# Hybrid decoder trunk on one core: the prompt's keys turned by token with VectorE blocks and small DMAs, final states at the end of each scan

## The chip, the cores and the metric

The kernel runs on one core of one Trainium2 chip. A core has five engines with a program each: TensorE (PE in the profile, its weight loads PEld), VectorE (DVE), ScalarE (ACT), GpSimd (POOL) and SyncE (SP). SP computes nothing here and only issues DMAs. The engines wait for each other and for DMAs through semaphores. The metric is the device time of one execution in microseconds (us), lower being better.

## The reference

One inference step of a single decoder layer, for a prompt of 256 tokens and for a group of 8 samples with 4 new tokens each (32 columns), so 288 tokens of width 2048 in fp32:

```python
x = x + 0.5 * rmsnorm(swiglu(rmsnorm(x, g[0]), ffn1_w_in, ffn1_w_out), g[1])
m, sg, sh = hybrid_mixer(rmsnorm(x, g[2]), ...)
x = x + rmsnorm(m, g[3])
x = x + 0.5 * rmsnorm(swiglu(rmsnorm(x, g[4]), ffn2_w_in, ffn2_w_out), g[5])
```

The mixer projects its input to the queries, keys, values and gates of 4 GLA heads (key width 128, value width 256) and 8 HGRN heads (128 and 128). Each head is a recurrence over the tokens with a decay per key element:

```python
# S_t = diag(exp(log_a_t)) S_{t-1} + k_t^T v_t ; o_t = q_t S_t
s_new = (jnp.exp(last)[..., None] * s
         + jnp.einsum('bhsd,bhsv->bhdv', ki * jnp.exp(last - cum), vi))
```

The prompt starts from a zero state and the samples from states that are read from memory. Outputs are the 288 tokens, the state of every head after the prompt, and the 8 new states of every head for the samples. For this document the second line matters: a head's state after the prompt is the product, over all 256 tokens, of the keys (each scaled by the decay from its token to the end) with the values.

## The kernel before

Nearly all of the time goes into products of weights with 288 columns. `Weights` loads every weight matrix once, in units of 128 x 1024 fp32 (512 KB), through SP into three buffers `raw`. ACT rounds a unit to fp32r (`wh`, L95) and DVE forms the rest (`wl`, L96). With the input split the same way into `xh` and `xl`, `block` makes three products of 128x128 weights with 288 columns for each piece: `xh*wh` (L520), `xl*wh` (L521), `xh*wl` (L522). Loads and splits run ahead of PE: three units may be loaded and four split before PE comes to them.

In the mixer a second stream of work lies between these products. `block` calls `tick` once for each of the 16 row tiles k of its input, and each tick takes one step of the oldest unfinished `scan`, a generator whose steps end at its `yield` statements. There are six scans of two heads each: two GLA scans, then four HGRN scans. A scan lies between the products of the blocks qk, v, hfq, hi and gate, as its ticks fall. The scheduler of the language may move an instruction within its engine's order a little; each engine then works strictly in that order.

A scan holds two heads a = 0, 1 with their queries, keys `k` (128 key elements on the partitions, 288 tokens along the row) and decay. In eight levels DVE multiplies decays into `k` and `Q` in place (`update`, L961 and L964), PE makes scores (L919 to L1017) and DVE or ACT put them into `Dg`. After the last level `k` holds each prompt key scaled to the end of the prompt. Then the second part begins, which the change touches:

- `key_t(a)` (L1085) turns the keys of head a: PE transposes the 256 prompt tokens in two products with the identity (L828) and the 32 sample tokens, kept three times side by side in `K3`, in a third (L829), all into one PSUM tile `tp_k`. PSUM tiles of this kind (`auxtile`) have three buffers.
- `key_e(a)` (L1090): ACT copies the prompt part to `kd`, which has tokens on the partitions (L1094), and ACT and DVE split the sample part to `ks` (L833, L835).
- `out(a)`: the prompt's output from scores and values (L1113 to L1117).
- for every nb samples `halve`, `apart` and `sample`: a state tile `s` is loaded by SP (L895, five buffers), split, multiplied by the queries (L1159), updated on DVE (L1163, from the product `sn`, L1151 or L1154) and stored by POOL (`out_dram<-s`, L1165).
- `final(a)` (L1121): the state after the prompt, two products of `kd` with the values (L1126), copied by ACT to `st` (one buffer, L1128) and stored by POOL (L1129). It is called in head a's first sample step.
- `inter_a`, `inter_b` (with the product `os<-sel`, L1177), `norm_a` and later `norm_b`, `norm_c` finish the outputs of a head.

POOL has little to do in this stretch: it issues the stores of `s` and `st`. SP's queue holds the weight loads and the loads of `s`, in one order; a load of `s` waits until the store of the tile five before it has landed. At the very end of the program the last FFN already turns tiles with DVE's 32x32 block transpose (`turn32`, L625, L627) and moves the blocks into place with DMAs (`move32`, L636, L640), issued by POOL and SP.

Of the kernel before, what the change touches and what calls it, by code (L numbers as in the profile page):

```python
# [9 lines left out]
F32 = mybir.dt.float32  # L10
# [6 lines left out]
P = 128  # L17
# [20 lines left out]
class Weights:  # L38
# [77 lines left out]
    def next(self):  # L116
        if self.used >= self.split:
            self.ahead()
        p = self.parts.pop(self.used)
        self.used += 1  # L120
        return p
# [3 lines left out]
def trunk_kernel(ctx, tc, x_prompt, x_sample, state_gla, state_hgrn, norm_gains, f1_in, f1_out, f2_in, f2_out,  # L125
# [615 lines left out]
    def mixer(pn, border):  # L741
        with ExitStack() as mx:
# [82 lines left out]
            def by_token(tp, src, src3):  # L825

                for t in range(2):
                    PE.transpose(tp[:, t * P:(t + 1) * P], src[:, t * P:(t + 1) * P], ident)  # L828
                PE.transpose(tp[0:96, TP:TP + P], src3, ident)  # L829
# [42 lines left out]
            def scan(d, Vt, V32, Vs, gla, ytile0, s0, sp_out, ss_out):  # L872
# [209 lines left out]
                put(LEVELS - 1, pss.pop(LEVELS - 1))  # L1082
                kds, bds, hls, sqs, pos, mss = {}, {}, {}, {}, {}, {}

                def key_t(a):  # L1085
                    tp = auxtile("tp_k")
                    by_token(tp, k[:, a, :], K3[:, a].rearrange("p n t -> p (n t)"))
                    return tp

                def key_e(a, tp):  # L1090

                    kd = sp[0].tile([P, 2, P], F32, name="kd", tag="kd")
                    ks = sp[0].tile([96, P], F32R, name="ks", tag="ks")
                    S.activation(kd, tp[:, 0:TP].rearrange("p (t c) -> p t c", c=P), AF.Copy)  # L1094
                    stack(ks, tp, 2 * TS)
                    kds[a] = kd, ks

                def apart(a, b0):

# [6 lines left out]
                def out(a):  # L1106
                    vc = Vt[:, :, a * dv:(a + 1) * dv]

                    po, ss = auxtile("o"), auxtile("os")
                    for j in range(nv):  # L1110
                        vj = vc[:, :, j * P:(j + 1) * P]
                        c0, c1, c2 = j * TP, j * TP + P, (j + 1) * TP
                        PE.matmul(po[:, c0:c1], vj[:, 0, :], Dg[:, 0, a, :], start=j == 0, stop=True, skip_group_check=True)  # L1113
                        PE.matmul(po[:, c1:c2], vj[:, 0, :], X[:, a, :], start=False, stop=False, skip_group_check=True)
                        PE.matmul(po[:, c1:c2], vj[:, 1, :], Dg[:, 1, a, :], start=False, stop=True, skip_group_check=True)
                        c0 = TP + j * TS
                        PE.matmul(ss[:, c0:c0 + TS], V32[:, a * dv + j * P:a * dv + (j + 1) * P], Ds[:, a, :],  # L1117
                                  start=j == 0, stop=False, skip_group_check=True)
                    pos[a] = po, ss

                def final(a):  # L1121

                    kd, vc = kds[a][0], Vt[:, :, a * dv:(a + 1) * dv]
                    ps = auxtile("st")
                    for t in range(2):
                        PE.matmul(ps[:, 0:dv], kd[:, t, :], vc[:, t, :], start=t == 0, stop=t == 1)  # L1126
                    st = tmp.tile([P, dv], F32, name="st", tag="st", bufs=1)
                    S.activation(st, ps[:, 0:dv], AF.Copy)  # L1128
                    G.dma_start(sp_out[a], st)  # L1129

                def halve(a, b0):

                    load_state()
                    s = states[a, b0]
                    for i in range(2):
                        hl = sp[0].tile([P, 512], F32R, name="hl", tag="hl", bufs=4)
                        v = hl.rearrange("p (b two c) -> p b two c", two=2, c=dv)
                        sv = s[:, i * nb // 2:(i + 1) * nb // 2, :]
                        with tc.issue_after(pn.behind[1]), tc.issue_after(pn.behind[2]):
                            S.activation(v[:, :, 0, :], sv, AF.Copy)  # L1140
                            V.tensor_tensor(v[:, :, 1, :], sv, v[:, :, 0, :].bitcast(F32), op=ALU.subtract)
                        hls.setdefault((a, b0), []).append(hl)
# [24 lines left out]
                def inter_a(a):  # L1167
                    ss = pos[a][1]
                    it = its[0]
                    S.activation(it[0:2 * TS, 0:dv], ss[0:2 * TS, 0:dv], AF.Copy)  # L1170
                    if not gla:
                        V.tensor_tensor(it[0:2 * TS, 0:dv], it[0:2 * TS, 0:dv], ss[0:2 * TS, dv:2 * dv], op=ALU.add)
# [7 lines left out]
                def norm_a(a):  # L1180
                    for j in range(nv):
                        yt = y[ytile0 + a * nv + j]
                        S.activation(yt[:, 0:TP], pos[a][0][:, j * TP:(j + 1) * TP], AF.Copy)
                        S.activation(yt[:, TP:T], pos[a][1][:, TP + j * TS:TP + (j + 1) * TS], AF.Copy)
                        sq = sqp.tile([P, T], F32, name="hsq", tag="sq")
                        S.activation(sq, yt, AF.Square)
                        if j == 1:
                            V.tensor_tensor(sq, sq, sqs[a], op=ALU.add)
                        sqs[a] = sq
                    h = sqp.tile([P, T], F32R, name="nh", tag="pn")  # L1190
                    l = sqp.tile([P, T], F32R, name="nl", tag="pn")
                    S.activation(h, sqs[a], AF.Copy)
                    V.tensor_tensor(l, sqs[a], h.bitcast(F32), op=ALU.subtract)
                    sqs[a] = h, l
# [18 lines left out]
                                               op0=ALU.mult, op1=ALU.mult)  # L1213

                tp = key_t(0)
                halve(0, 0)
                yield
                out(0)
                key_e(0, tp)
                apart(0, 0)  # L1220
                yield
                for a in range(2):
                    for b0 in range(0, NB, nb):
                        if b0 + nb < NB:
                            apart(a, b0 + nb)
                            halve(a, b0 + nb)
                        if b0 == 0:
                            final(a)
                        sample(a, b0)
                        if a == 0 and b0 == nb:  # L1230
                            tp = key_t(1)
                        yield
                        if a == 0 and b0 == nb:
                            key_e(1, tp)
                    if a == 0:
                        apart(1, 0)
                        halve(1, 0)
                    inter_a(a)
                    yield
                    inter_b(a)  # L1240
                    norm_a(a)
                    later.append([lambda: None, lambda: None, lambda a=a: norm_b(a), lambda a=a: norm_c(a)])
                    yield
                    if a == 0:
                        out(1)
                        yield

            gens, later = [], []
# [228 lines left out]
```

## Time and profile before

| what | us |
|---|---|
| median of three runs | 2281.41 (2281.22 to 2283.21) |
| the profiled execution | 2280.79 |
| its span from first to last instruction | 2279.0 |
| PE busy | 2264.1 (99%) |
| DVE busy | 1420.8 (62%) |
| ACT busy | 1034.4 (45%) |
| POOL busy | 115.8 (5%) |

The profile is one execution of the program, and its times count from its first instruction. Busy time is the union of an engine's instructions; matmuls overlap, since one starts while the one before it still runs, so the distance from start to start tells what a matmul costs, and its duration does not. A row of a group gives the number of its instructions behind an x. Waits are put down to what ended them. "DMA to landing" is the time from a DMA's issue until its data and its semaphore have arrived. The scans lie between about 918 and 1280 us.

### The profile page before, as it was taken

The numbers are of one execution on the slowest core, as the hardware profiler recorded it, in microseconds if no ns is written. First come the engines' busy times: TensorE is split into PE (matmuls) and PEld (weight loads), VectorE is DVE, ScalarE is ACT, GpSimd is POOL, SyncE is SP. The second block draws the span as 40 slices with busy tenths as digits, with TensorE's granted clock in tenths as the row PEclk, the third lists the DMA queues.
The fourth block names the chain that finished last, engine by engine and source line by source line (L and its number), as shares of the span: only waits on it lengthen the run. The fifth ranks groups of instructions, "written<-read, shape, count | busy, mean of one in ns | idle before, by whom it ended". The sixth has DMA issues, their size and how long they took to land.

```text
span 2279.0 us, 42090 instructions
## 1 busy us (share of the span) xinstructions
PE 2264.1 (99%) x17164; PEld 2252.0 (99%) x17164; DVE 1420.8 (62%) x2375; ACT 1034.4 (45%) x1603; POOL 115.8 (5%) x204
## 2 busy tenths in 40 slices
PE   9999999999999999999999999999999999999998
PEld 9999999999999999999999999999999999999997
DVE  7545545554555468889889754954555455545546
ACT  6443333333334346556656654644333333333344
POOL 0000000000000002001000000260000000000003
PEclk9999999999999999999999999999999999999999
DMA  7555555555555545456465554475555555555555
GB/s 218 169 165 165 165 167 165 166 166 167 167 167 185 166 158 163 139 171 198 144 183 159 167 183 160 141 203 169 165 166 164 166 167 166 167 167 167 167 163 151
DMA packets 228801, 382.42 MB, mean 168 GB/s; under 512 B 24018, under 2 KB 63936, under 8 KB 228608
## 3 DMA queue, kind: packets, MB, share of 16 engines
q1 hardware_dynamic: 219088, 366.27, 50.7%
q0 software_dynamic: 7344, 13.29, 2.1%
q8 instruction: 134, 2.20, 0.4%
q10 hardware_dynamic: 2176, 0.18, 0.1%
q14 instruction: 59, 0.48, 0.1%
HBM read 363.75 MB, written 11.80 MB: 165 GB/s over the span
## 4 chain that ended last, share of the span: by engine, by line
PE 94%; DVE 3%; DMA 1%; ACT 1%; issue 0%; DVEq 0%; SPq 0%; ACTq 0%
PE gate L522 9%; PE gate L520 9%; PE gate L521 9%; PE up L522 8%; PE up L520 8%; PE up L521 8%; PE out L521 8%; PE out L522 8%; PE out L520 8%; PE hfq L520 2%; PE hfq L522 2%; PE mo L522 1%; PE mo L520 1%; PE mo L521 1%; PE hfq L521 1%; PE v L520 1%
## 5 line engine op out<-in xcount | busy, mean ns | idle before, releaser
L96 DVE TENSOR_TENSOR wl<-raw,wh 128x1024 fp32r<-128x1024 f32 (+1 forms) x674 | 821.6, 1219 | 621.0 <-ACT wh L95 619.1
L95 ACT ACTIVATE wh<-raw 128x1024 fp32r<-128x1024 f32 (+1 forms) x674 | 711.6, 1057 | 1017.6 <-PE gate L521 315.8
L522 PE MATMUL gate<-xh,wl 128*128 128x288 f32 x1660 | 489.0, 295 | 0.2 <-DVE wl L96 0.2
L520 PE MATMUL gate<-xh,wh 128*128 128x288 f32 x1660 | 488.9, 296 | 0.3 <-ACT wh L95 0.3
L521 PE MATMUL gate<-xl,wh 128*128 128x288 f32 x1660 | 485.5, 295 | 0.0
L522 PE MATMUL out<-hh,wl 128*128 128x288 f32 x1408 | 415.1, 295 | 0.9 <-DVE wl L96 0.9
L521 PE MATMUL out<-hl,wh 128*128 128x288 f32 x1408 | 415.7, 295 | 0.0
L522 PE MATMUL up<-xh,wl 128*128 128x288 f32 x1408 | 415.0, 295 | 0.0
L520 PE MATMUL up<-xh,wh 128*128 128x288 f32 x1408 | 414.8, 295 | 0.1
L521 PE MATMUL up<-xl,wh 128*128 128x288 f32 x1408 | 414.6, 294 | 0.0
L520 PE MATMUL out<-hh,wh 128*128 128x288 f32 x1408 | 413.7, 294 | 0.0
L522 PEld LDWEIGHTS gate<-xh,wl 128*128 128x128 f32 x1660 | 311.5, 188 | 0.6 <-DVE wl L96 0.6
L520 PEld LDWEIGHTS gate<-xh,wh 128*128 128x128 f32 x1660 | 310.9, 188 | 1.2 <-ACT wh L95 0.5
L521 PEld LDWEIGHTS gate<-xl,wh 128*128 128x128 f32 x1660 | 310.4, 188 | 0.2
L522 PEld LDWEIGHTS out<-hh,wl 128*128 128x128 f32 x1408 | 264.7, 188 | 1.1 <-DVE wl L96 1.1
L520 PEld LDWEIGHTS out<-hh,wh 128*128 128x128 f32 x1408 | 264.6, 188 | 0.0
L520 PEld LDWEIGHTS up<-xh,wh 128*128 128x128 f32 x1408 | 264.1, 188 | 0.5 <-ACT g L590 0.3
L521 PEld LDWEIGHTS out<-hl,wh 128*128 128x128 f32 x1408 | 264.4, 188 | 0.0
L521 PEld LDWEIGHTS up<-xl,wh 128*128 128x128 f32 x1408 | 264.2, 188 | 0.1
L522 PEld LDWEIGHTS up<-xh,wl 128*128 128x128 f32 x1408 | 264.2, 188 | 0.0
L671 DVE TENSOR_TENSOR y<-out,y 128x288 f32<-128x288 f32 x288 | 121.4, 452 | 98.9 <-PE out L522 95.9
L520 PE MATMUL hfq<-xh,wh 128*128 128x288 f32 x256 | 77.5, 303 | 0.0
(381 smaller groups left out, 2598.2 us busy)
## 6 DMA issues: line engine op xcount, KB each, us to landing
raw<-in_ffn_w_in_dram SPq DMA_DIRECT2D x351, 512.0 KB, 3.4
raw<-in_ffn_w_out_dram SPq DMA_DIRECT2D x176, 512.0 KB, 3.5
raw<-in_mix_w_in_dram SPq DMA_DIRECT2D x64, 512.0 KB, 3.7
raw<-in_mix_w_in_dram SPq DMA_DIRECT2D x96, 256.0 KB, 3.2
raw<-in_mix_w_out_dram SPq DMA_DIRECT2D x32, 512.0 KB, 3.7
out_dram<-s POOLq DMA_DIRECT2D x32, 256.0 KB, 3.5
s<-in_state_gla_dram SPq DMA_DIRECT2D x16, 256.0 KB, 4.2
s<-in_state_hgrn_dram SPq DMA_DIRECT2D x16, 256.0 KB, 3.6
```

The lines of the kernel that those rows point to most:

```text
L95: i1 = self.nc.scalar.activation(h[:, c], raw[:, c], AF.Copy).ins
L96: i2 = self.nc.vector.tensor_tensor(l[:, c], raw[:, c], h[:, c].bitcast(F32), op=ALU.subtract).ins
L520: yield lambda: PE.matmul(dst, w[0][:, c:c + P], parts[0], start=start, stop=False)
L521: yield lambda: PE.matmul(dst, w[0][:, c:c + P], parts[1], start=False, stop=False)
L522: yield lambda: PE.matmul(dst, w[1][:, c:c + P], parts[0], start=False, stop=stop)
L671: V.tensor_tensor(y[k], ps, y[k], op=ALU.add)
```

## The change

The prompt part of the keys is no longer turned by PE. After the last level one DVE instruction (L1087 of the changed kernel) transposes each 32x32 block of `k[:, :, 0:256]` in its place, for both heads. A block then holds its own tokens on its partitions, but stands in the wrong place of the 128x128 tile. 32 DMAs per scan, issued by POOL (L1093), copy the blocks to `kd`, which now holds both heads and has one buffer: for each head and each group of 32 key elements four DMAs, each of 32 partitions x 2 x 32 elements (64 pieces of 128 B, 8 KB). `keys_by_token` issues four of them at each of its steps, and `scan` takes one such step behind most of its own. `key_t` keeps only the transpose of the sample part (L1098); `key_e` loses ACT's copy to `kd`. `final(0)` moves behind `inter_a(1)` and `final(1)` behind `norm_a(1)`, the last steps of the scan.

```diff
+                def keys_by_token():
+
+                    V.transpose(k[:, :, 0:TP], k[:, :, 0:TP])
+                    kd = sp[0].tile([P, 2, 2, P], F32, name="kd", tag="kd", bufs=1)
+                    for a in range(2):
+                        for b in range(4):
+                            src = k[b * TS:(b + 1) * TS, a, 0:TP].rearrange("p (t q c) -> p t q c", t=2, q=4)
+                            for c in range(4):
+                                G.dma_start(kd[c * TS:(c + 1) * TS, a, :, b * TS:(b + 1) * TS], src[:, :, c, :])
+                            yield kd
+
                 def key_t(a):
                     tp = auxtile("tp_k")
-                    by_token(tp, k[:, a, :], K3[:, a].rearrange("p n t -> p (n t)"))
+                    PE.transpose(tp[0:96, TP:TP + P], K3[:, a].rearrange("p n t -> p (n t)"), ident)
                     return tp
 
                 def key_e(a, tp):
 
-                    kd = sp[0].tile([P, 2, P], F32, name="kd", tag="kd")
                     ks = sp[0].tile([96, P], F32R, name="ks", tag="ks")
-                    S.activation(kd, tp[:, 0:TP].rearrange("p (t c) -> p t c", c=P), AF.Copy)
                     stack(ks, tp, 2 * TS)
-                    kds[a] = kd, ks
+                    kds[a] = None, ks
...
-                        PE.matmul(ps[:, 0:dv], kd[:, t, :], vc[:, t, :], start=t == 0, stop=t == 1)
+                        PE.matmul(ps[:, 0:dv], kd[:, a, t, :], vc[:, t, :], start=t == 0, stop=t == 1)
...
                 tp = key_t(0)
+                keys = keys_by_token()
+                kd = next(keys)
                 halve(0, 0)
                 yield
+                next(keys)
                 out(0)
...
-                        if b0 == 0:
-                            final(a)
                         sample(a, b0)
                         if a == 0 and b0 == nb:
                             tp = key_t(1)
+                        next(keys, None)
                         yield
...
                     inter_a(a)
+                    if a == 1:
+                        final(0)
+                    next(keys, None)
                     yield
                     inter_b(a)
                     norm_a(a)
+                    if a == 1:
+                        final(1)
                     later.append([lambda: None, lambda: None, lambda a=a: norm_b(a), lambda a=a: norm_c(a)])
+                    next(keys, None)
                     yield
                     if a == 0:
                         out(1)
+                        next(keys, None)
                         yield
```

In the order in which the changed program stands, POOL's DMAs of a scan come as runs of key DMAs with the stores of `s` between them: 15, a store, 16, a store, 1 in the first GLA scan; 14, 9, 9 in the second; 8, 4, 18, 2 in the first HGRN scan; then 11, 10, 11; 11, 11, 10; and 8, 4, 20. Every DMA of POOL uses one of eight semaphores in turn, so that an issue waits until the eighth DMA before it has landed. Each `final` waits on PE for all eight of them.

More of the change, by code (lines that the diff above doesn't have):

```diff
@@ L1121, in final @@
                 def final(a):
-                    kd, vc = kds[a][0], Vt[:, :, a * dv:(a + 1) * dv]
+                    vc = Vt[:, :, a * dv:(a + 1) * dv]
                     ps = auxtile("st")
                     for t in range(2):
-                        PE.matmul(ps[:, 0:dv], kd[:, t, :], vc[:, t, :], start=t == 0, stop=t == 1)
+                        PE.matmul(ps[:, 0:dv], kd[:, a, t, :], vc[:, t, :], start=t == 0, stop=t == 1)
                     st = tmp.tile([P, dv], F32, name="st", tag="st", bufs=1)
```

## The prediction

> **What bounds the kernel now.** I read the page's busy times first, then the table of stretches inside the scans, then PE's waits.
>
> ```profile
> span 2279.0 us, 42090 instructions
> PE 2264.1 (99%) x17164; PEld 2252.0 (99%) x17164; DVE 1420.8 (62%) x2375; ACT 1034.4 (45%) x1603; POOL 115.8 (5%) x204
> ```
> ```profile
> 1080.00:1120.00 40.00, 40.00 (x308) 39.00 (x307) 33.63 (x84) 27.21 (x68) 4.11 (x6) 1.00 0.53 162
> 1200.00:1240.00 40.00, 40.00 (x304) 39.32 (x304) 39.26 (x95) 30.19 (x72) 4.11 (x6) 1.00 0.56 163
> ```
> ```profile
> PE out L522 <- DVE wl L96: 0.9, 1, 0.9
> PE sc L983 <- DVE R L976: 0.7, 1, 0.7
> PE tp_v L828 <- DVE y L849: 0.3, 1, 0.3
> ```
>
> The columns of the second fence are stretch, its length, then busy time (and count) of PE, PEld, DVE, ACT, POOL, granted clock, DMA share, GB/s. PE is never idle in these two stretches of the scans, at a granted clock of 1.00, while DVE is nearly full in the second one (39.26 of 40 us). The third fence shows how little PE waits at all. So the time is what PE has to do, plus any wait that PE is given; other engines count only when they make it wait.
>
> **The change part by part.**
>
> *The transposes that go.* The order in time around the first `tp_k` gives their price, the group's row gives their duration:
>
> ```profile
> 944.65 0.30 PE L522 MATMUL qk<-xh,wl 128*128 128x288 f32 x1
> 944.78 0.38 PE L828 MATMUL tp_k<-ident,k_g 128*128 128x128 f32 x2
> 945.00 0.27 PE L829 MATMUL tp_k<-ident,acc 128*96 128x128 f32 x1
> ```
> ```profile
> L828 PE MATMUL tp_k<-ident,k_h x16: 270/272/301, 1084.5 to 1258.2; 128*128 128x128 f32 x16
> L828 PE MATMUL tp_k<-ident,k_g x8: 270/272/273, 944.8 to 1027.1; 128*128 128x128 f32 x8
> ```
>
> A matmul starts while the one before it still drains. The pair of L828 holds PE from 944.78 to 945.00, 0.22 us, though each one lasts 0.272 us. There are 24 of them, 12 pairs: 12 x 0.22 = 2.6 us less on PE. L829 stays. The Trainium skill's page "TensorE: Matmul & The Clock Gate" (Part 4: PE-mode transpose) gives about 275 ns for a 128x128 transpose inside a kernel, and by that price the term would be 6.6 us. The trace's duration agrees with it (272 ns); the trace's distance of starts, 0.11 us, does not.
>
> *ACT's copy that goes, DVE's transpose that comes.*
>
> ```profile
> L1094 ACT ACTIVATE kd<-tp_k x12: 363/368/386, 945.9 to 1258.8; 128x256 f32<-128x256 f32 x12
> L625 DVE STREAM_TRANSPOSE b<-x x16: 398/404/446, 1450.9 to 1523.3; 128x256 f32<-128x256 f32 x16
> ```
>
> ACT loses 12 x 0.368 = 4.4 us; it is idle a quarter to a third of these stretches, so that is worth nothing by itself. DVE's block transpose of 256 columns took 0.404 us; one of 512 is about twice that, 0.81 us, six times 4.9 us. It stands behind the last decay step of `k`. What hides it are the weight units that stand split ahead of PE: PE's waits name `wl` with 0.9 us once, outside the scans. Without that cover it would cost up to 4.9 us.
>
> *The key DMAs on POOL.* 6 x 32 = 192 issues come. The nearest rows are the DMAs of blocks in the last FFN and POOL's stores in the scans:
>
> ```profile
> L640 POOL DMA_DIRECT2D xS<-bs x16: 563/563/563, 1461.2 to 1535.0; - x16
> L636 POOL DMA_DIRECT2D xT<-b x64: 585/585/605, 1457.8 to 1534.4; - x64
> L1129 POOL DMA_DIRECT2D out_dram<-st x12: 553/553/571, 951.8 to 1273.7; - x12
> L1165 POOL DMA_DIRECT2D out_dram<-s x32: 710/750/752, 952.6 to 1277.9; - x32
> ```
>
> A key DMA has fewer pieces (64) than those of `xS` (128), so I take 0.56 us. POOL computes nothing there; what counts is who stands behind it. First the stores of `s` are late: in the second GLA scan these stood here.
>
> ```profile
> 1026.94 0.71 POOL L1165 DMA_DIRECT2D out_dram<-s  x1 [1.93 <-DVE k_h L1326]
> 1030.51 0.72 POOL L1165 DMA_DIRECT2D out_dram<-s  x1 [2.86 <-DVE s L1163]
> 1035.87 1.50 POOL L1165 DMA_DIRECT2D out_dram<-s  x2 [4.64 <-DMA raw<-in_mix_w_in_dram]
> 1013.83 0.43 DVE L964 TENSOR_TENSOR k_g<-k_g,F 128x256 f32<-128x256 f32 x1 [0.87 <-PE sc L1003]
> ```
>
> The keys are turned at 1015.1. After 14 key DMAs the first store still leaves at 1026.9; nine more then hold POOL until 1032.7 and nine more until 1038.5, so the second and third stores leave 2.2 and 2.6 us later. SP then waits longer to reload such tiles, with the weight loads behind it:
>
> ```profile
> SPq L63 <- DVE wl L96: 73.9, 23, 9.3
> SPq L895 <- DMA out_dram<-s: 69.2, 22, 7.8
> ```
>
> Already SP waits 22 times for stores, up to 7.8 us, and PE does not wait for a weight in the scans. SP also waits 23 times for a buffer that DVE frees, so the loads are early. I take nothing, and keep 7.8 us (three stores at 2.6) as the upper end.
>
> *The final states, which now wait for DMAs.* This is the term that can eat the gain. PE works in order, so a `final` whose key blocks have not landed holds everything behind it. `final(1)` stands next to the last `os<-sel` of its scan. How long have the DMAs? From the end of the last update of `k` to that place, for the second GLA scan (its start above) and the four HGRN scans:
>
> ```profile
> 1083.80 0.42 DVE L964 TENSOR_TENSOR k_h<-k_h,F 128x256 f32<-128x256 f32 x1
> 1130.35 0.42 DVE L964 TENSOR_TENSOR k_h<-k_h,F 128x256 f32<-128x256 f32 x1
> 1195.66 0.43 DVE L964 TENSOR_TENSOR k_h<-k_h,F 128x256 f32<-128x256 f32 x1 [0.31 <-PE sc L1003]
> 1250.30 0.42 DVE L964 TENSOR_TENSOR k_h<-k_h,F 128x256 f32<-128x256 f32 x1
> ```
> ```profile
> 1058.46 0.53 PE L1177 MATMUL os<-sel,it 128*128 128x32 f32 x4
> 1107.56 0.30 PE L1177 MATMUL os<-sel,it 128*128 128x32 f32 x2
> 1157.68 0.30 PE L1177 MATMUL os<-sel,it 128*128 128x32 f32 x2
> 1221.95 0.30 PE L1177 MATMUL os<-sel,it 128*128 128x32 f32 x2
> 1279.57 0.30 PE L1177 MATMUL os<-sel,it 128*128 128x32 f32 x2
> ```
> ```profile
> DMA to landing us min/median/max: 1.8/2.5/3.9
> DMA to landing us min/median/max: 1.9/3.7/5.5
> ```
>
> The last two rows are those of `st` in the scans and of `xT` in the last FFN. In the first HGRN scan the keys are ready at 1084.22, transposed at 1085.0. 32 issues of 0.56 and the three stores between them of 0.75 are 20.2 us: the last issue begins at 1104.6 and lands 1.8 to 3.9 us later, at 1106.5 to 1108.5, in the middle 1107.1. PE comes to `final(1)` at about 1106.5: 1107.56 less the two pairs of this scan (0.43) and some five products of the block (0.13 each) that the changed order puts behind it. That is a wait of 0.0 to 2.0 us, and 0.6 us with `st`'s median landing, the row of the same stretch; I take 0.7. With the slowest `xT` it is 3.6 us. The other three have 25.7, 24.6 and 27.6 us from turned keys to `final(1)` (0.4 taken off for the pairs), against 20.2 - 0.6 + 2.5 = 22.1, so their DMAs land 2 us or more ahead; the second GLA scan has 43 us, and the first is built the same. `final(0)` needs only the first 16 DMAs.
>
> *Two smaller things.* Each `final` waits for eight semaphores, 4 or 5 extra waiting instructions on PE, some 53 in all:
>
> ```profile
> L828 PEldq EVENT_SEMAPHORE  x16: 51/51/1149, 943.9 to 1256.7; - x16
> ```
>
> At 0.051 us each they are 2.7 us at most. But PE's queue works ahead of its array: one such wait of 1.149 us shows up as no wait of that size among PE's waits (`tp_v`, 0.3). I take 0. And `st` has one buffer: with the two finals close together, ACT's second copy waits for the first store, 0.56 + 2.5 us, less the 3 to 11 ACT instructions that stand between. What is queued behind is ACT's work for `norm_a` and the next `wh`; the split units cover it. I take 0, at most 1 us in each of the four HGRN scans.
>
> *The sum.* -2.6 (transposes) + 0.7 (the first HGRN scan's wait) = -1.9 us. Against the profiled execution's 2280.79 that is 2278.9. The median of the runs shown lies 0.6 us above that execution, so the forecast is 2281.4 - 1.9 = 2279.5 us. About 0.2% (4.6 us) is what a measurement of this kernel can tell from no change, so this counts as the same. This case's own range goes from all of the gain and some of PE's small waits too (-3.5) to the upper ends of the final's wait and `st` (-2.6 + 3.6 + 1 = +2): 2277.9 to 2283.4.
>
> **The rivals.**
>
> *Slower: the key DMAs land late.* With eight semaphores POOL issues no faster than one DMA in an eighth of a landing. Up to 4.5 us of landing (8 x 0.56) the issue sets the pace; above it, the landing L does, and a scan's 32 blocks take 4L + 2.25 + L. The four HGRN scans have 21.5, 25.7, 24.6 and 27.6 us. At L = 5.0 that is 27.25 us, with waits of 5.8, 1.6, 2.7 and 0: 10.0 us, net +7.4, 2289. It decides from about L = 4.8 on. For it speaks the longest `xT` (5.5 us) and the DMA share of 0.53 to 0.56; against it `st`'s 2.5 in the same stretch. A slower issue would do the same: at the 0.75 us of the stores, 32 x 0.75 + 2.25 - 0.75 + 2.5 = 28.0 us, waits 6.5, 2.3, 3.4 and 0.4, net +10.0, 2291. Against that, the issues of `s` and `st` never spread by more than 0.042 us with DVE 84 to 98% busy. Chance 0.16. The Trainium skill's page "SBUF — State Buffer" (Who interferes with whom) says that VectorE in a two-port mode keeps GpSimd from writing the descriptors of its DMAs, which would be such a slower issue. The rows just named show no such hold.
>
> *Slower: SP's queue.* The stores' delay passes through the reloads to the weights, as above: +7.8 - 1.9, 2287.3. It needs the longest wait, 7.8 + 2.6 = 10.4 us, to outlast what is loaded and split ahead. Against it: PE waits for no weight there. Chance 0.07.
>
> *Faster: a transpose costs its duration.* 24 x 0.272 = 6.5 us, 2274.9. The starts at 0.22 us for two speak against it. With the chance that PE's other small waits in the scans (0.7 and 0.3 above) also go, 0.13.
>
> *Nothing is left of it.* Waiting instructions and `st` cost their upper ends: -1.9 + 2.7 + 4 = +4.8 at most, in the middle about 2282. Chance 0.08, most of it within the same 0.2%.
>
> **How the numbers follow.** The likeliest case has 0.56. Same: 0.56 and 0.07 of the last rival, 0.63; slower: 0.16 + 0.07 + 0.01 = 0.24; faster: 0.13. The range leaves out most of the case at 2274.9 and the longer waits of the DMA case, under 2 in 10: 2276.5 to 2288.
>
> **What would show it.** `tp_k` of L828 is gone, L1098 follows a product by 0.13 us; L1087 takes 0.8 us; L1093 0.56 us, landing under 4 us. PE's waits name `st` with DMA `kd` once or not at all, in the first HGRN scan, under 2 us. It would be wrong if `st` waits in several scans, if L1093 issues at more than 0.65 us or lands after 4.8, or if PE begins to wait for `wl` or `wh` between 1000 and 1280 us.

## The result and the profile after

| | before | after |
|---|---|---|
| median of 11 runs each, same chip | 2280.99 us | 2286.75 us |
| lowest and highest | 2279.49 to 2283.72 | 2284.85 to 2288.37 |
| span of the profiled execution | 2279.0 us | 2285.1 us |

The ratio is 1.0025, with a 95% interval of 1.0017 to 1.0033: the changed kernel is slower by 5.8 us, a quarter of a per cent. The forecast was 1.9 us faster, counted as the same. The time is inside the range (2276.5 to 2288), but only in the part that was added for the slower rivals: the likeliest case, 2277.9 to 2283.4, did not come.

The page's busy times and PE's waits of the changed kernel (a wait's row ends with us in total, times, longest):

```profile
span 2285.1 us, 42280 instructions
PE 2264.0 (99%) x17140; PEld 2250.7 (98%) x17140; DVE 1423.8 (62%) x2381; ACT 1030.1 (45%) x1591; POOL 218.4 (10%) x396
```
```profile
PE st L1135 <- DMA kd<-k_h: 3.9, 1, 3.9
PE gate L520 <- DVE z L1389: 1.4, 1, 1.4
PE tp_v L828 <- DVE y L849: 0.9, 1, 0.9
PE sn L1160 <- DVE s L1172: 0.8, 1, 0.8
```

PE has 24 matmuls fewer, and waits that were not there before. The largest is `final(1)` of the first HGRN scan. The stretches around it (same columns as in the prediction) show a second cost right behind it:

```profile
1107.00:1111.20 4.20, 0.42 (x4) 0.21 (x2) 3.74 (x8) 1.66 (x6) 4.11 (x7) 1.00 0.30 83
1111.20:1115.60 4.40, 4.25 (x21) 4.28 (x22) 0.55 (x2) 1.91 (x4) 0.55 (x1) 0.61 0.89 261
1115.60:1120.00 4.40, 4.40 (x36) 4.26 (x34) 3.13 (x7) 1.76 (x4) 0.00 (x0) 1.00 0.78 241
```

PE stands still for 3.9 us. Then the granted clock is 0.61 on the mean of the next 4.4 us, and 21 matmuls run there where 36 run in the stretch behind. At a clock of 0.61, 4.4 us do the work of 2.7, so 1.7 us more are lost.

POOL in the same scan, in order of time (in brackets the idle time before, and what ended it; "issue" where the profile names nothing):

```profile
1087.01 4.29 POOL L1093 DMA_DIRECT2D kd<-k_h  x8 [26.01 <-issue]
1091.29 0.78 POOL L1174 DMA_DIRECT2D out_dram<-s  x1
1092.07 2.14 POOL L1093 DMA_DIRECT2D kd<-k_h  x4
1094.20 0.78 POOL L1174 DMA_DIRECT2D out_dram<-s  x1
1094.98 4.26 POOL L1093 DMA_DIRECT2D kd<-k_h  x8
1099.92 2.28 POOL L1093 DMA_DIRECT2D kd<-k_h  x4 [0.69 <-DMA kd<-k_h]
1104.74 3.19 POOL L1093 DMA_DIRECT2D kd<-k_h  x6 [2.53 <-issue]
1107.92 0.78 POOL L1174 DMA_DIRECT2D out_dram<-s  x1
1108.70 1.08 POOL L1093 DMA_DIRECT2D kd<-k_h  x2
```

From 1087 to 1110 us POOL issues one DMA behind the other, with two pauses of 0.69 and 2.53 us. The third store of `s` leaves at 1107.92 and the last key DMA at 1109.24. Before the change POOL issued the same store at 1103.36, and SP the load of `s` that follows it at 1106.16 (1110.98 now):

```profile
1103.36 0.75 POOL L1165 DMA_DIRECT2D out_dram<-s  x1 [2.69 <-DVE s L1163]
```
```profile
1106.16 0.37 SPq L895 DMA_DIRECT2D s<-in_state_hgrn_dram  x1
```

Two more engines wait for POOL's stores, as the waits of ACT and of SP's queue say:

```profile
ACT st L1137 <- DMA out_dram<-st: 9.0, 5, 4.4
SPq L895 <- DMA out_dram<-s: 80.4, 18, 12.2
```

ACT's copy to the one `st` buffer waits up to 4.4 us for the store of the `st` before it, and SP's longest wait for a store of `s` has grown from 7.8 to 12.2 us. PE's waits name neither. Read alone, this profile says: 3.9 us for the key DMAs, 1.7 for the clock, the rest small. The experiments show that this is only the first of several ways.

### The profile page after: what moved, and what is told of

It reads as the page before. It is cut to its first block, busy times and chain, and to the rows that moved or that the text cites. A ratio compares the mean times of both kernels' runs of the same rounds, so it can differ in the third digit from the quotient of the medians.

```text
span 2285.1 us, 42280 instructions
## 1 busy us (share of the span) xinstructions
PE 2264.0 (99%) x17140; PEld 2250.7 (98%) x17140; DVE 1423.8 (62%) x2381; ACT 1030.1 (45%) x1591; POOL 218.4 (10%) x396
## 4 chain that ended last, share of the span: by engine, by line
PE 89%; DVE 4%; DMA 3%; POOL 2%; issue 1%; ACT 1%; DVEq 0%; SPq 0%; ACTq 0%; POOLq 0%
PE gate L520 9%; PE gate L522 9%; PE gate L521 9%; PE up L522 8%; PE up L520 8%; PE up L521 8%; PE out L521 8%; PE out L522 8%; PE out L520 8%; POOL kd L1093 2%; PE mo L522 1%; PE mo L520 1%; PE mo L521 1%; PE hfq L520 1%; PE hfq L522 1%
## 5 line engine op out<-in xcount | busy, mean ns | idle before, releaser
L636 POOL DMA_DIRECT2D zT<-b x24 | 14.0, 588 | 709.6 <-DVE bs L627 709.4
```

The lines of the kernel that those rows point to most:

```text
L636: queues[n % len(queues)].dma_start(dst[q * TS:(q + 1) * TS, 4 * g:4 * g + 4, :, cols].rearrange("p k t c -> p (k t) c"), b32[rows, q])
```

## The experiments

Each run is compared with runs of the kernel before on the same chip, whose medians were 2279.7 to 2280.8 us. With 4 to 11 runs of a kernel and 15 to 22 of the kernel before, such a ratio is known to 0.1 to 0.15%, 2 to 3.5 us.

### Parts of the change alone, on the kernel before

The transposes only: PE's pair and ACT's copy go, nothing else.

```diff
-                    by_token(tp, k[:, a, :], K3[:, a].rearrange("p n t -> p (n t)"))
+                    PE.transpose(tp[0:96, TP:TP + P], K3[:, a].rearrange("p n t -> p (n t)"), ident)
-                    S.activation(kd, tp[:, 0:TP].rearrange("p (t c) -> p t c", c=P), AF.Copy)
-                        PE.matmul(ps[:, 0:dv], kd[:, t, :], vc[:, t, :], start=t == 0, stop=t == 1)
+                        PE.matmul(ps[:, 0:dv], k[:, a, t * P:(t + 1) * P], vc[:, t, :], start=t == 0, stop=t == 1)
```


> The kernel before without PE's transposes of the prompt's keys and without ACT's copy of them; `final` stays where it was and multiplies `k` as it lies. Left out: the turning of the prompt's keys, so the states after the prompt are wrong ones. It is the price of the 24 transposes alone. Theory (distance of starts, 0.22 us a pair): 2.6 us less than before, 2278.4. Rival (their duration, 0.27 us each): 6.5 us less, 2274.5. Rival (they lie where PE would wait anyway): no change, 2281.0.

Measured: 2278.56 us against 2280.75, ratio 0.9990 (0.9981 to 0.9999), 2.2 us less (0.2 to 4.3). The distance of starts (2.6) fits, the duration (6.5) does not.

VectorE's part only: the block transpose is added, into the dead tile `Q`.

```diff
+                V.transpose(Q.rearrange("p a t -> p (a t)")[:, 0:2 * TP].rearrange("p (a t) -> p a t", a=2), k[:, :, 0:TP])
```


> The kernel before with one addition: after the last level VectorE transposes the blocks of the prompt's keys into the dead tile `Q`, six times; nobody reads them, PE and ACT turn the keys as before. It is the price of VectorE's part alone. Theory (VectorE is full in the third HGRN scan, where the kernel with 16 DMAs and own halves of `st` lost 2 to 3 us by late `hl`, `s` and `z`): 1 to 3 us more than before, with PE waiting for DVE `s`, `hl` or `z` between 1200 and 1240 us. Rival (hidden by the units split ahead, as predicted): no change within 0.7 us.

Measured: 2280.60 against 2280.15, 1.0002 (0.9993 to 1.0011). No cost can be told. The theory named 1 to 3 us; the interval reaches up to 2.5 us, but PE's waits of this run name none of DVE's `s`, `hl` or `z` between 1200 and 1240 us, so nothing speaks for VectorE's part.

The finals only: `final(0)` behind `inter_a(1)`, `final(1)` behind `norm_a(1)`.

```diff
-                        if b0 == 0:
-                            final(a)
...
                     inter_a(a)
+                    if a == 1:
+                        final(0)
...
                     norm_a(a)
+                    if a == 1:
+                        final(1)
```


> The kernel before with nothing changed but the place of the finals: `final(0)` behind `inter_a(1)`, `final(1)` behind `norm_a(1)`, as in the changed kernel. Transposes and ACT's copy of the keys stay, there are no key DMAs. Theory (two finals close together with one `st` buffer cost up to 2.2 us): 1.0 to 2.2 us more than before, 2282.0 to 2283.2, with ACT's `st` copy waiting for `out_dram`. Rival (all of the loss comes from waiting for DMAs): no change, 2281.0 within 0.5.

Measured: 2282.39 against 2280.75, 1.0008 (0.9999 to 1.0017), 1.6 us more. That is as the theory had it, though the interval just reaches no change. ACT waits here too, without any key DMA:

```profile
ACT st L1128 <- DMA out_dram<-st: 6.4, 6, 2.1
```

### One wait cut at a time

First ACT's wait: the two heads of an HGRN scan get the two halves of `st`, a tile that is twice as wide as they need.

```diff
-                    st = tmp.tile([P, dv], F32, name="st", tag="st", bufs=1)
+                    if gla or a == 0:
+                        sts[0] = tmp.tile([P, 2 * P], F32, name="st", tag="st", bufs=1)
+                    st = sts[0] if gla else sts[0][:, a * P:(a + 1) * P]
```


> One change to the changed kernel: in the HGRN scans the two heads' `st` are the two halves of one tile of 256 columns (it had that size already for the GLA scans), so that ACT's second copy no longer waits for the first store. Theory (the single `st` buffer costs time by ACT's late copies, DVE's late evictions and PE's missing PSUM buffers): the waits of ACT's `st` copy on `out_dram` in the HGRN scans (4.4, 1.8, 0.5 us) go, PE's wait `gate` on DVE `z` (1.4 us) goes, and the time falls by 1.4 to 2.2 us, from 2286.8 to about 2285. Rival (ACT's wait is covered, the 1.4 us come from DVE's own load): no change, 2286.8 within 0.5.

Measured: 2287.44 against 2280.75, 1.0029 (1.0017 to 1.0040). Nothing came back that could be told from noise. PE still waits for the keys in the first HGRN scan. A second wait of `final(1)` has come up in the third one, 2.6 us, put down to the store that shares its eight semaphores. There landings reached 6.0 us and held POOL's issues. It is the rival of late landings, in one scan of one execution:

```profile
PE st L1135 <- DMA kd<-k_h: 4.1, 1, 4.1
PE st L1135 <- DMA out_dram<-st: 2.6, 1, 2.6
```
```profile
1221.98 1.07 POOL L1093 DMA_DIRECT2D kd<-k_h  x2 [1.23 <-DMA kd<-k_h]
1224.20 1.60 POOL L1093 DMA_DIRECT2D kd<-k_h  x3 [1.14 <-DMA out_dram<-s]
```

Then PE's wait: `final` multiplies the block-transposed `k` in its place, and nobody reads `kd`.

```diff
-                        PE.matmul(ps[:, 0:dv], kd[:, a, t, :], vc[:, t, :], start=t == 0, stop=t == 1)
+                        PE.matmul(ps[:, 0:dv], k[:, a, t * P:(t + 1) * P], vc[:, t, :], start=t == 0, stop=t == 1)
```


> One change to the changed kernel: `final` multiplies the block-transposed `k` itself instead of `kd`, so that PE waits for no key DMA; all 192 DMAs are still issued. Left out: the right arrangement of the keys, so the states after the prompt are those of other keys. Theory (4.2 us of waiting in the first HGRN scan and 1.7 us of half clock behind it): 5.9 us less, 2280.9, and granted clock 1.00 in the first HGRN scan. Rival 1 (the half clock has another cause than the wait): 4.2 us less, 2282.6, with the clock still 0.5 somewhere near 1112. Rival 2 (POOL's issues themselves slow the scans, by the stores and SP's queue): less than 3 us gained, 2284 or more.

Measured: 2290.09 against 2280.75, 1.0039 (1.0026 to 1.0051): with the wait gone the kernel got no faster, if anything slower. The theory and the first rival fell; the second rival has its number, but what stands behind it had first to be found. PE's waits and ACT's instructions say where the time is now:

```profile
PE sc L919 <- ACT R L911: 6.2, 1, 6.2
```
```profile
1112.49 0.28 ACT L1137 ACTIVATE st<-st 128x128 f32<-128x128 f32 x1 [5.61 <-DMA out_dram<-st]
1116.40 1.06 ACT L95 ACTIVATE wh<-raw 128x1024 fp32r<-128x1024 f32 x1 [2.01 <-DMA raw<-in_mix_w_in_dram]
1117.36 0.44 ACT L911 ACTIVATE R<-Q 128x288 f32<-128x288 f32 x1
```

ACT's second `st` copy stands 5.61 us behind the first store, which POOL comes to behind its key DMAs. `R`, the input of the next scan's first scores, is written in two instructions that stand behind that copy on ACT, and PE's scores, at 1117.86, wait for the second, `R<-Q`. Between them a weight split waits 2.01 us more, for `raw`. So two waits stand one behind the other here, and the one that ends last is for weights. The clock is halved too, for 10.2 us where it was 3.4 in the changed kernel; PE works 6.4 of them, which loses 3.2 us.

Both cut together:

> The changed kernel with both ways cut by which a late key DMA reaches PE: `final` multiplies the block-transposed `k` (PE waits for no key DMA) and the two heads of an HGRN scan have their own halves of `st` (ACT's second copy waits for no store). All 192 key DMAs are still issued by POOL. Left out: the right arrangement of the keys, so the states after the prompt are those of other keys. Theory (the loss comes by these two ways only, and each alone hides behind the other): the price of the transposes is left, 2.2 to 2.6 us under before: 2278.2 to 2279.5, no PE wait over 2 us, no stretch of half clock. Rival (the issues on POOL cost something by themselves, by the stores of `s`, SP's queue or VectorE): 2281 or more.

Measured: 2286.50 against 2280.08, 1.0032 (1.0019 to 1.0044), still 6.4 us more than before. The theory of two ways fell; the rival, the stores of `s` and SP's queue, came out. PE's wait, then ACT, SP and POOL of this kernel in order of time:

```profile
PE sc L919 <- ACT R L911: 4.9, 1, 4.9
```
```profile
1115.18 1.06 ACT L95 ACTIVATE wh<-raw 128x1024 fp32r<-128x1024 f32 x1 [6.38 <-DMA raw<-in_mix_w_in_dram]
1116.14 0.44 ACT L911 ACTIVATE R<-Q 128x288 f32<-128x288 f32 x1
```
```profile
1095.90 0.37 SPq L63 DMA_DIRECT2D raw<-in_mix_w_in_dram  x1
1109.50 0.37 SPq L895 DMA_DIRECT2D s<-in_state_hgrn_dram  x1
1109.97 0.48 SPq L63 DMA_DIRECT2D raw<-in_mix_w_in_dram  x1
```
```profile
1103.01 3.19 POOL L1093 DMA_DIRECT2D kd<-k_h  x6 [3.43 <-issue]
1106.19 0.78 POOL L1176 DMA_DIRECT2D out_dram<-s  x1
```

SP issues nothing for 13.6 us: its next load of `s` needs the tile whose store POOL comes to only at 1106.19, behind the key DMAs. The weights stand behind that load on SP; ACT waits 6.38 us for the next unit, and `R` stands behind that unit on ACT. It is the wait for `raw` that the run before already ended with. So the same late POOL reaches PE at nearly the same place (from 1107 or 1112 us) by three ways: the keys, the store of `st`, and the store of `s` with SP's weights behind it. PE's wait there was 3.9 us in the changed kernel, 6.2 with the first cut and 4.9 with the first two.

### The place in POOL's queue

To move the DMAs behind the stores of `s`, the steps of `keys_by_token` were first called at the end of the scan, on top of both cuts:

> As the kernel with both ways cut (`final` reads the block-transposed `k`, the HGRN heads have their own halves of `st`), and the 32 key DMAs of a scan, still issued by POOL, stand behind all stores of `s` of their scan. Left out: the right arrangement of the keys; nobody reads `kd`. Theory (the third way: key DMAs ahead of the stores of `s`, SP's loads of `s` behind those stores, weights behind those loads): SP's longest wait for a store falls from 12 us or more back to about 8, ACT waits no 6 us for `raw` in the first HGRN scan, and the time is that of the kernel without transposes: 2278.0 to 2279.8. Rival (192 DMAs of 64 pieces disturb loads or VectorE wherever they stand): 2282 or more.

Measured: 2290.04 against 2279.66, 1.0043 (1.0031 to 1.0056). This did not test what it was meant to: the scheduler put the DMAs ahead of the stores again (POOL issues the first at 1083.85, the first store of `s` at 1087.07). ACT waits 8.39 us for `raw`, and SP's longest wait for a store of `s` is 15.4 us, where it was 12.2 in the changed kernel:

```profile
SPq L895 <- DMA out_dram<-s: 77.8, 22, 15.4
```

So each DMA was tied behind the scan's last store on POOL:

```diff
+                    stored[0] = G.dma_start(sp_out[a], st).ins
...
+                                with tc.issue_after(stored[0]):
+                                    G.dma_start(kd[c * TS:(c + 1) * TS, a, :, b * TS:(b + 1) * TS], src[:, :, c, :])
```


> As the kernel with both ways cut (`final` reads the block-transposed `k`, own halves of `st`), with the 32 key DMAs of each scan tied behind the store of that scan's last `st`, so that they stand in POOL's queue behind all its stores; in the kernel before this one the scheduler had put them ahead of the stores again. Left out: the right arrangement of the keys; nobody reads `kd`. Theory (the third way is POOL's queue order: key DMAs, then the store of `s`, then SP's load of the next `s`, then the weights behind it): SP's longest wait for a store is about 8 us again, ACT does not wait over 2 us for `raw` in the first HGRN scan, 2278.0 to 2280.5. Rival (192 DMAs of 64 pieces cost their 6 us wherever they stand, as load on the DMA engines or on VectorE): 2283 or more.

Measured: 2277.94 against 2280.15, 0.9991 (0.9983 to 1.0000). The 192 DMAs are all there, their pieces and their landings as before (median 2.9 us). What differs from the run at 2286.50 is their place in the queue and, with it, their time: in the first HGRN scan POOL now issues them from 1106.5 to 1128.3 us. 8.6 us are gone. This is the same 2.2 us under the kernel before as without any key DMA, though the interval just reaches no change. SP's wait for stores and PE's at the place:

```profile
SPq L895 <- DMA out_dram<-s: 63.9, 20, 7.7
```
```profile
1107.00:1111.20 4.20, 4.20 (x34) 4.20 (x32) 4.20 (x9) 2.77 (x5) 2.92 (x7) 1.00 0.94 306
```

The other direction: all 32 in one run ahead of the stores, in the changed kernel (the `yield kd` moves out of the loop).

> One change to the changed kernel: the 32 key DMAs of a scan are issued in one run at the scan's first step, ahead of the stores that stand between them now. Theory (what counts is when POOL comes to the last of 32 DMAs): the two to three stores of 0.78 us are no longer ahead of it, so in the first HGRN scan the last issue is 2.3 us earlier, PE's wait falls from 3.9 to about 1.6 us, no half clock, and `st`'s store is as late as it was: 2283 to 2285. Rival (the steps of the scan pace the issues): the wait goes altogether, 2281 or less. Rival (the eight semaphores pace them, at a landing of 4 us or more): no gain, 2286 or more.

Measured: 2295.64 against 2280.08, 1.0070 (1.0057 to 1.0083). All expectations missed: I had counted what the keys win and not what the stores lose. The third has a number that would cover it, but not its mechanism: the first 26 issues took 0.53 us each. In the first HGRN scan the four stores of `s` leave in one row behind the keys, and ACT's split `hl` of a later state tile waits for SP's load of it, with the copy of `st` and `R` behind it:

```profile
1102.63 3.19 POOL L1093 DMA_DIRECT2D kd<-k_h  x6 [2.55 <-issue]
1105.82 3.02 POOL L1175 DMA_DIRECT2D out_dram<-s  x4
```
```profile
1113.67 0.42 ACT L1150 ACTIVATE hl<-s 128x256 fp32r<-128x256 f32 x1 [4.23 <-DMA s<-in_state_hgrn_dram]
```

That is a fourth way from POOL's late stores to PE. PE's `final` waits in three of the four HGRN scans, and the clock is halved three times.

### Fewer DMAs, larger pieces, another queue

16 DMAs a scan: VectorE transposes into `Q` with the two heads 256 columns apart, so that one DMA moves a block column of both.

```diff
+                    kb = Q.rearrange("p a t -> p (a t)")[:, 0:2 * TP]
+                    V.transpose(kb.rearrange("p (a t) -> p a t", a=2), k[:, :, 0:TP])
...
+                    for b in range(4):
+                        src = kb[b * TS:(b + 1) * TS].rearrange("p (n q c) -> p n q c", n=4, q=4)
+                        for c in range(4):
+                            G.dma_start(kv[c * TS:(c + 1) * TS, :, b * TS:(b + 1) * TS], src[:, :, c, :])
+                        yield kd
```


> The changed kernel with 16 key DMAs per scan: VectorE transposes the blocks into the dead tile `Q` with the heads 256 columns apart, so one DMA moves a block column for both heads (128 pieces, 16 KB). Theory (it is the number of issues): 0.56 us each, 9 us in place of 17.2, the last key block of the first HGRN scan lands before 1102, PE waits for no `kd`, the first `st` store is not behind key DMAs; no half clock. 2279 to 2281.5, the upper end by ACT's copies with one `st` buffer as in the moved finals alone (+1.6). Rival (it is the number of pieces or the load of the DMA engines): issues of 0.9 us or more, or landings above 5 us, and 2285 or more.

Measured: 2284.02 against 2280.08, 1.0020 (1.0012 to 1.0029). No wait for `kd` and no halved clock as expected, but more than the forecast: ACT's `st` copy of the first HGRN scan still waits 4.0 us, and `R` behind it costs PE 2.5 us.

```profile
1109.98 0.28 ACT L1138 ACTIVATE st<-st 128x128 f32<-128x128 f32 x1 [3.99 <-DMA out_dram<-st]
```

With own halves of `st` as well:

> The kernel with 16 key DMAs per scan, and the two heads of an HGRN scan in their own halves of `st`. Theory: both costs gone, the price of the transposes is left: 2.2 to 2.6 us under before, 2278.2 to 2279.5, ACT's `st` copies wait less than 1 us in the HGRN scans. Rival (with key DMAs early the `st` buffer is covered anyway): the same time as with 16 DMAs alone.

Measured: 2280.41 against 2280.08, 1.0001 (0.9992 to 1.0010), 3.6 us less than with one `st`, the only difference between the two: the buffer is worth that much once nothing else hides it. It is the kernel before's time, 1 to 2 us above the forecast.

Pieces of 512 B, with the four groups of 128 tokens innermost in `Q` and in `kd`:

> Own halves of `st`, 16 key DMAs per scan of 32 pieces of 512 B: VectorE transposes into `Q` with the four 128-token groups innermost, `kd` has the same order and PE reads it with a step of four elements. Against the 16 DMAs of 128 pieces of 128 B it changes the size of the pieces alone (and makes six block transposes into twenty-four of a quarter). Theory (what is left of the cost is the place of the issues in POOL's queue): no change against that kernel's 2280.4, within 1 us. Rival (the small pieces slow landings and weight loads): 1 to 2 us less, 2278.4 to 2279.4, with landings under 3 us. Rival (PE reads weights with a step slower, or VectorE writes with a step slower): more than 2281.5.

Measured: 2282.29 against 2279.66, 1.0012 (1.0003 to 1.0020). The landings are as before (2.6 us at the median either way), so the size of the pieces doesn't show in them. The second rival came, and PE's half of it is in the trace: PE is busy 3.6 us more (2266.0 against 2262.4), and its loads of weights with a step of four elements are slower, as the tile's groups show. VectorE's half, more and smaller transposes, was not told apart:

```profile
L1135 PEld LDWEIGHTS st<-Vh,kd x32: 308/329/330, 1102.4 to 1279.6; 128*128 128x128 f32 x32
```

They took 0.190 to 0.192 us without the step.

The same 16 DMAs issued by ACT:

> As the kernel with 16 key DMAs of 512 B pieces, issued by ACT in place of POOL. POOL's queue is then that of before: stores of `s` and `st` wait for no key DMA. ACT pays 16 issues per scan and waits for VectorE's transpose. Theory (POOL's queue holds what is left of the cost, ACT has a quarter free): 2278.0 to 2279.5. Rival (ACT's issues delay `wh` and the evictions as the late `st` copies did): 2281 or more.

Measured: 2300.26 against 2279.66, 1.0092 (1.0077 to 1.0108), the rival's side and far beyond it. POOL's queue is free, and now the splits of the weights stand behind the DMAs:

```profile
ACT wh L95 <- DMA kd<-Q: 22.2, 3, 8.6
ACT wh L95 <- DMA raw<-in_mix_w_in_dram: 19.7, 13, 4.3
```

### A version with the right states

The key DMAs behind the scan's last store of `s`, and the finals ten ticks later, in the next scan:

```diff
+                        slow.append([lambda: None] * 10 + [lambda: final(0), lambda: final(1)])
```


> A version that computes the right states with what the runs so far point to: PE makes no transposes of the prompt's keys, the 32 key DMAs of a scan are tied behind the store of its last `s` in POOL's queue, and the two finals are put off by ten ticks (about 23 us) into the next scan, so that PE waits for no key DMA; own halves of `st`. Theory (POOL's queue order was the whole loss): as with the keys behind the stores and unread, 2277.5 to 2279.0, PE names no `st` wait above 0.5 us. Rival (values and `kd` held longer, or the finals in the next scan's levels, take PSUM buffers or make PE wait): 2280 or more, with PE, ACT or DVE waiting for `st` or for `Vt`.

Measured: 2282.83 against 2280.23, 1.0008 (0.9999 to 1.0017), in runs from 2279.2 to 2287.6. Its profiled execution is the slowest of them. There the last scan's `final(1)` comes to PE just when POOL has issued the last key DMA, and waits, and the clock is halved behind it:

```profile
PE st L1136 <- issue: 3.0, 1, 3.0
```
```profile
1302.20:1304.00 1.80, 1.80 (x11) 1.80 (x11) 1.27 (x3) 1.28 (x4) 0.56 (x1) 0.62 0.00 0
1304.00:1306.00 2.00, 2.00 (x10) 2.00 (x9) 0.83 (x3) 0.62 (x3) 0.00 (x0) 0.50 0.44 142
```

With fourteen ticks in the HGRN scans:

> One change to the version with deferred finals: in the HGRN scans the finals are put off by fourteen ticks, not ten; in the last scan ten ticks had brought `final(1)` to PE at 1298.7 us, when the last key DMA had just been issued, and PE waited 3.2 us there. Theory: that wait goes and with it what comes behind it; 2278.0 to 2280.0, PE names no `st` wait above 0.5 us. Rival (the execution with that wait was one of several kinds, and what varies lies elsewhere): the median stays at 2281 or more.

Measured: 2278.69 against 2279.80, 0.9994 (0.9985 to 1.0003). That is the theory's range, and PE names no `st` wait; SP's longest wait for a store is 7.7 us. It is some 7 us faster than the changed kernel by their ratios to the kernel before, and not to be told from the kernel before itself: the whole prize of this change is 2.2 us.

## Why the prediction went wrong, step by step

- **Transposes, -2.6.** Fits: -2.2 (+-2) alone. The duration's price (6.5) is refuted.
- **DVE's transpose and ACT's copy, 0.** Not refuted: DVE's part alone cost 0.45 us, inside the error (-1.6 to 2.5). One transpose took 0.70 to 0.71 us, not 0.81.
- **Issue time, 0.56.** Right: 0.539 us at the median, 0.694 at most, by the tile's groups. The landings, 2.9 us at the median, stayed far from the 4.8 at which the first rival begins:

```profile
L1093 POOL DMA_DIRECT2D kd<-k_h x128: 539/539/694, 1087.0 to 1282.0; - x128
DMA to landing us min/median/max: 1.6/2.9/5.1
```

- **`final(1)` in the first HGRN scan, +0.7 (0 to 2, 3.6 at most).** Mis-sized: 3.9 (4.1 in the kernel with own halves of `st`), and 1.7 of halved clock behind it, which no term had. The last issue was forecast at 1104.6 and came at 1109.24. Its parts: the first issue came at 1087.01 and not at 1085.0, since the last decay step of `k` ended 1.1 us later than before, a split `ks` went ahead of the transpose, and 0.6 us passed between the transpose's end and the issue; POOL stood 0.69 us for a semaphore and 2.53 us for nothing that the profile shows; the issues and stores themselves were 0.6 us shorter than forecast. The landing took 2.0 us, inside the forecast's 1.8 to 3.9. PE came to `final(1)` at 1107.4, 0.9 us later than forecast. In the other three HGRN scans PE did not wait for keys in the changed kernel, as said. (Their times leave out the five products, 0.65 us, that the first scan's takes off; their margin of 2 us or more bears it.)
- **One `st` buffer, 0 (at most 1 in each HGRN scan).** Wrong in its cover. I named what stands behind the copy on ACT and said that the units split ahead hide it. But `R` stands there too, which the next scan's scores need at once. It is worth 3.6 us with 16 key DMAs; the moved finals cost 1.6 us without any, at the edge of the error and with the move itself in it.
- **POOL's stores and SP, 0 (rival 7.8, chance 0.07).** This is the step that failed most. I sized the delay in the second GLA scan, where the third store of `s` is 2.6 us late, and argued from PE's waits that weights are early. In the first HGRN scan the third store stands behind 30 key DMAs, SP's load of `s` moved from 1106.16 to 1109.50 with both cuts, and that is where the weights are scarce: without key DMAs, in the run with the transposes alone taken away, PE already waits there:

```profile
PE sc L919 <- ACT R L911: 1.3, 1, 1.3
```

  By its place in the queue, and the time that goes with it, the same work costs 8.6 us (2286.50 to 2277.94).

So the forecast erred less in the size of one wait than in its form: I summed terms one by one, each with its cover, where three of them had one cause, POOL's lateness, and one place. None of the three is the loss by itself, and the profile after named only the one that came last. What remains open is how the 5.8 us of the changed kernel divide among the ways; cutting one does not measure it. Open too is how much of POOL's lateness is its unexplained pause, which stands ahead of the third store in every kernel with 32 key DMAs but those with the keys behind the stores.

## What to carry to other kernels

When a change puts work into an in-order queue that had been idle, price the items behind it, in the stretch where they are latest and not where they are easiest to see, and follow each to the engine that stands behind it. A wait that the profile names can hide an equal one behind it; cut both, and if the time stays, look for a third. If added DMAs are needed late, put them behind what others wait for, and give their reader the time.

## What the runs showed of the hardware

**The clock.** PE's granted clock fell to 0.5 behind each wait of 3.0 us or more (3.0, 3.2, 3.8, 3.9, 4.1, 4.9, 6.2, 6.9). It stayed at 1.00 behind 2.6 us in the kernel with own halves of `st`, and yet fell behind 2.0 us in the second HGRN scan of the kernel with all DMAs in one run. The length of the wait is not what tells them apart. A low stretch lasts 3.41 us, or two or three times that (6.8 and 10.2), so I cut the traces into pieces of 3.41 us, counted from a change of the clock. First the 2.0 us, then the 2.6:

```profile
1163.30:1166.71 3.41, 1.39 (x13) 1.28 (x12) 1.18 (x4) 1.63 (x4) 0.45 (x1) 1.00 0.80 244
1166.71:1170.13 3.42, 3.42 (x17) 3.42 (x16) 1.52 (x2) 0.73 (x3) 0.10 (x1) 0.50 0.91 256
```
```profile
1226.04:1229.45 3.41, 1.75 (x15) 1.64 (x13) 3.15 (x9) 2.10 (x6) 1.83 (x3) 1.00 1.01 338
1229.45:1232.86 3.41, 2.48 (x19) 2.51 (x20) 1.72 (x4) 1.29 (x4) 0.55 (x1) 1.00 0.33 98
```

The 2.0 us lie in one piece, and the next is at 0.5; the 2.6 us are split between two, and the clock stays at 1.00. A full piece has about 28 matmuls. In the traces of all 17 kernels, up to the last 15 us of the program, ten pieces at full clock had 13 or fewer, and each was followed by a clock of 0.5, one of them with no wait above 1.6 us in it (the DMAs issued by ACT); no piece with 15 or more was. So what a wait costs depends on where it falls in these pieces. The Trainium skill's page "TensorE: Matmul & The Clock Gate" (Part 1: The HAM clock gate) halves the clock after an idle window of about 3.4 us, with windows that run freely. The windows agree. That a window must be idle does not: PE still worked 1.39 us of the one above.

**POOL's pauses.** In the first HGRN scan POOL stood 2.5 to 3.4 us before a key DMA with no releaser named, in every kernel that issues 32 key DMAs there among or ahead of the stores (2.53, 2.55, 3.43 in the rows above), and 2.2 to 2.6 us in those that issue them behind the stores. Counted from the program's start it is always POOL's 129th DMA, the 25th key in the changed kernel, the 27th with all in one run, the 21st behind the stores of `s` and `st`. With 16 key DMAs of 128 pieces a pause of 1.7 us stands before the 102nd in its place. So it goes by what POOL has issued so far and not by the time. Its cause was not tried.

**A step in the weights.** Loading 128x128 fp32 weights with a step of four elements took 0.329 us in place of 0.190 to 0.192.
